# Encoder trunk: four plain columns and nine pairs in the second to fourth feed-forwards, and the residual's sums closer together

## The chip, the cores and the metric

One core of a Trainium2 chip. The time is the device time of one execution in microseconds; the time before is the median of three runs, 2351.93 us (2351.7 to 2353.02).

## The reference

Two layers on a sequence of 512 positions with 1024 channels. Each layer adds a half-step feed-forward, a mixer (state space in layer 0, neighbourhood attention in layer 1), a second half-step feed-forward and a gated input embedding. So there are four feed-forwards, called the first to the fourth here, and only they are changed:

```python
def swiglu(x, w_gu, w_down):                 # w_gu 1024 x 5632, w_down 2816 x 1024
    g, u = jnp.split(x @ w_gu, 2, axis=-1)
    return (jax.nn.silu(g) * u) @ w_down

for i in range(DEPTH):                       # DEPTH = 2
    h = h + 0.5 * swiglu(rmsnorm(h, ffn1_norm[i]), ffn1_w_gu[i], ffn1_w_down[i])
    ...                                      # the mixer
    h = h + 0.5 * swiglu(rmsnorm(h, ffn2_norm[i]), ffn2_w_gu[i], ffn2_w_down[i])
    ...                                      # the gated embedding
```

## The kernel before, in words

The residual h lives in eight tiles of 128 channels by 512 positions. Every float32 matrix product is made of three matmuls: a value is split into a high part (a cast by ScalarE) and a low part (a subtraction by VectorE), and high x high, low x high and high x low are added up in PSUM (`gemm`, line 263). Weights come in units of 128 x 1024: a load on SyncE's queue into one of four raw buffers (`wr`), the cast `wh` (line 218) and the rest `wl` (line 220). `unit` (line 255) keeps up to three split units ready.

The hidden width of 2816 is 22 columns of 128, f=0 to f=21. The kernel computes them in two ways.

*Plain columns* (`gate_up`, line 382). One column takes two units, gate and up, of eight times three matmuls with 512 positions each. Its activation (`activate`, line 413) is a product with the norm's factor R for the gate (VectorE, line 415), a SiLU on ScalarE (416), the same product for up (418), the product of both on GpSimd (419), and a split (ScalarE 286, VectorE 287). R does not stand at the start: the matmuls work on the residual times the gain, and the sum of squares becomes R while TensorE is at the first columns. In the second to fourth feed-forwards R is there within f=1, in the first one within f=2.

*Pairs* (`block`, line 474). Two columns are made of seven half-sized products (a fast 2 x 2 scheme in place of eight), called blocks 0 to 6 here; a product is 24 matmuls with 256 positions (lines 483 to 485). It needs weights that are added up beforehand (lines 240, 243, 245, 251 on VectorE, for each pair) and sums of the residual, made once in each feed-forward by `sums(kk)` (line 432) for the four slices kk = 0 to 3. A slice takes h[kk] and h[kk+4], multiplies both by gain and R (line 437, twice), splits the parts (446 and 447, 286 and 287, 467 and 468) and forms their differences (462 to 465). Block 0 needs line 447's result of all four slices, slice by slice; block 1 needs line 468's.

*Down.* The hidden columns are grouped in chunks. While the products of a chunk run, the downs of the chunk before it are put between them (`ffn_order`, line 47): for each of eight output tiles a unit of weights as wide as the chunk, its matmuls, and an addition to h (line 546).

The columns before the change are chunks (0, 6), (6, 10), (10, 14), (14, 18), (18, 22), in all four feed-forwards: f=0 to 5 are plain, the rest are eight pairs. One slice of sums goes behind each plain column from the one on in which R is there; from f=4 on all that are left go at once. So the second to fourth feed-forwards have the slices behind f=1, 2, 3 and 4, and the first behind f=2, 3 and, two of them, f=4. The loads and splits of weights follow a list in program order (`plan`, line 143). The first pair's four weight blocks and their sums stand in it with the last three plain units (line 161).

The instructions of every engine are put in their final order by a scheduler when the kernel is built; the engines run them in that order.

Of the kernel before, what the change touches and what calls it, by code (L numbers as in the profile page):

```python
# [14 lines left out]
P = 128  # L15
# [3 lines left out]
DEPTH = 2  # L19
FF = 2816  # L20
NF = FF // P
CHUNKS = ((0, 6), (6, 10), (10, 14), (14, 18), (18, 22))
PLAIN = CHUNKS[0][1]
HT = T // 2
EPS = 1e-6
NH = 32
# [19 lines left out]
VAR = (0, 1, 1, 2)  # L46


def ffn_order():

    for f in range(PLAIN):
        yield "plain", f
    for c in range(1, len(CHUNKS)):
        a, b = CHUNKS[c]
        blocks = [(p, i) for p in range(a // 2, b // 2) for i in range(7)]
        d = 0
        for n, (p, i) in enumerate(blocks):
            yield "block", p, i  # L60
            while d < KD and (d + 0.5) * len(blocks) <= KD * (n + 1):
                yield "down", c - 1, d
                d += 1
    yield "between",
    for d in range(KD):
        yield "down", len(CHUNKS) - 1, d


@with_exitstack
def trunk(ctx, tc, A, out):  # L70
    nc = tc.nc
    v, s, g, te, sy = nc.vector, nc.scalar, nc.gpsimd, nc.tensor, nc.sync
# [70 lines left out]
    def plan():  # L143

        for i in range(stop):
            l, w = divmod(i, 4)
            if w in (0, 2):
                gu, gw, dn = [A[f"w_{x}{1 + w // 2}"][l] for x in ("gu", "gw", "dn")]  # L150

                def ahead(p, i_):
                    if i_ == 0:
                        yield "g", [gw[p - PLAIN // 2, x, y] for x, y in ((1, 0), (0, 0), (1, 1), (0, 1))]
                    yield "s", (p, i_)

                for what, *a in ffn_order():
                    if what == "plain":
                        for x in range(2):
                            yield "u", gu[a[0], x]  # L160
                            n = 2 * a[0] + x - (2 * PLAIN - 3)
                            if n >= 0:
                                yield from ahead(PLAIN // 2, n)
                    elif what == "block":
                        yield "o", a
                        if a[1] >= 4 and a[0] < NF // 2 - 1:
                            yield from ahead(a[0] + 1, a[1] - 4)
                    elif what == "down":
                        b = CHUNKS[a[0]]
                        yield "u", dn[a[1], :, b[0] * P:b[1] * P]  # L170
                    elif w == 2:
                        for n in range(2):
                            yield "u", A["w_proj"][l, n]
            elif w == 3:
                for n in range(KD):
                    yield "u", A["w_gate"][l, n]
            elif l % 2 == 0:
                for n in range(65):
                    yield "u", A["w_in"][n]
                for x in range(2):  # L180
                    for d in range(KD):
                        yield "u", A["w_out"][d, :, x * 1024:(x + 1) * 1024]
            else:
                for n in range(24):
                    yield "u", A["w_qkv"][n]
                for d in range(KD):
                    yield "u", A["w_ao"][d]

    todo = list(plan())

    loads = [x for what, a in todo if what in "gu"
# [34 lines left out]
    def prep_next():  # L226
        item = next(todo, None)
        if item is None:
            return False
        what, a = item  # L230
        if what == "u":
            split_raw(*take())
        elif what == "g":
            group[:] = [take()[0] for _ in range(4)]
        elif what == "s":
            p, i = a
            a21, a11, a22, a12 = group
            if i == 0:
                blocks[p] = {0: a11, 2: a21, 3: wide(), 4: a12, 6: a22}
                v.tensor_add(out=blocks[p][3], in0=a21, in1=a22)  # L240
            elif i == 1:
                blocks[p][1] = blocks[p][5] = wide()
                v.tensor_sub(out=blocks[p][1], in0=blocks[p][3], in1=a11)
            else:
                v.tensor_sub(out=a21, in0=a11, in1=a21)
        else:
            p, i = a
            b = blocks[p]
            split_raw(b[i], 1024)
            if i == 1:  # L250
                v.tensor_sub(out=b[5], in0=b[4], in1=b[5])
        top_up()
        return True

    def unit():
        while len(ready) < 3 and prep_next():
            pass
        return ready.pop(0)

    def part(xp, x, cols):  # L260
        return xp[x][:, cols] if isinstance(xp, tuple) else xp[:, x, cols]

    def gemm(pt, w, pairs, first=True, last=True, off=0, cols=slice(0, T), behind=False):
        hi, lo = w
        n = len(pairs)
        for k, xp in enumerate(pairs):
            sl = slice((off + k) * P, (off + k + 1) * P)
            m = te.matmul(out=pt, lhsT=hi[:, sl], rhs=part(xp, 0, cols), start=first and k == 0, stop=False)  # L268
            if behind and k == 0:
                tc.keep_in_program_order(m)  # L270
            te.matmul(out=pt, lhsT=hi[:, sl], rhs=part(xp, 1, cols), start=False, stop=False)  # L271
            te.matmul(out=pt, lhsT=lo[:, sl], rhs=part(xp, 0, cols), start=False, stop=last and k == n - 1)  # L272
# [103 lines left out]
    def ffn(norm, nxt, between=None, first=None):  # L376
        R = [None]
        mids = {}
# [146 lines left out]
            v.tensor_sub(out=hl[1][:, :, c], in0=x, in1=hl[0][:, :, c])  # L525

        made, left = None, [0, 1, 2, 3]
        for what, *a in ffn_order():
            if what == "plain":
                gate_up(a[0])  # L530
                while left and R[0] is not None:
                    sums(left.pop(0))
                    if a[0] < 4:
                        break
            elif what == "block":
                if between and a == [CHUNKS[-1][0] // 2, 0]:
                    next(between)
                block(*a)
            elif what == "between":
                made = between and next(between)  # L540
            else:
                c, d = a
                last = c == len(CHUNKS) - 1
                pt = mm_bank() if last else px_bank()
                gemm(pt, unit(), [mids[f] for f in range(*CHUNKS[c])])
                v.scalar_tensor_tensor(out=h[d], in0=pt, scalar=0.5, in1=h[d], op0=ALU.mult, op1=ALU.add)
                if last:
                    nxt(d)
                    if d == 2 and made is not None:
                        made[1]()  # L550
# [677 lines left out]
    n = Norm(C_G1)  # L1228
# [56 lines left out]
    for i in range(stop):  # L1285
        l, w = divmod(i, 4)
        last = i == stop - 1
        m = None if last else Norm(gains[i + 1], (lambda: md(F32R)) if w == 2 else xa)
        nxt = done if last else m.prep
        if w == 0:  # L1290
            ffn(n, nxt, first=first if i == 0 else None)
        elif w == 1:
            (ssd if l % 2 == 0 else attention)(n, nxt)
        elif w == 2:
            pp = ffn(n, nxt, ple_proj(l))
        else:
            ple(l, n, pp, nxt)
        n = m


def prepare(inp):
    import numpy as np

    def units(w):
        k, n = w.shape[0] // P, w.shape[1] // P
        return w.reshape(k, P, n, P).transpose(2, 1, 0, 3).reshape(n, P, k * P)

    f = {k: np.asarray(a) for k, a in inp.items()}
    o = {}
    o["x"] = f["x"][0].T.reshape(KD, P, T).transpose(1, 0, 2)  # L1310
    p = f["p"][:, 0].reshape(DEPTH, 8, 64, 2, P)
    o["p"] = p.transpose(0, 4, 3, 2, 1).reshape(DEPTH, P, 2, T)
    for i in (1, 2):
        gu = f[f"ffn{i}_w_gu"]
        gu = np.stack([units(gu[l]).reshape(2, NF, P, 1024).transpose(1, 0, 2, 3) for l in range(DEPTH)])
        o[f"w_gu{i}"] = gu[:, :PLAIN]

        gw = gu[:, PLAIN:].reshape(DEPTH, (NF - PLAIN) // 2, 2, 2, P, 2, 512).transpose(0, 1, 3, 5, 4, 2, 6)
        o[f"w_gw{i}"] = gw.reshape(DEPTH, (NF - PLAIN) // 2, 2, 2, P, 1024)
        o[f"w_dn{i}"] = np.stack([units(f[f"ffn{i}_w_down"][l]) for l in range(DEPTH)])  # L1320
    o["w_gate"] = np.stack([units(f["ple_w_gate"][l]) for l in range(DEPTH)])
    o["w_proj"] = np.stack([units(f["ple_w_proj"][l]).reshape(2, 4, P, 256).transpose(0, 2, 1, 3).reshape(2, P, 1024)
                            for l in range(DEPTH)])
# [31 lines left out]
    i = np.arange(P)  # L1355
# [15 lines left out]
    b = np.full((16, 3, 16, 8, 32, 8), NEG, np.float32)  # L1371
# [26 lines left out]
```

## Time and profile before

| | |
|---|---|
| median of 3 runs | 2351.93 us |
| profiled execution, its own time | 2352.96 us |
| span of the profiled execution | 2351.2 us |
| TensorE (PE) busy | 2327.4 us, 99% |
| VectorE (DVE) busy | 1805.7 us, 77% |
| ScalarE (ACT) busy | 1111.8 us, 47% |
| GpSimd (POOL) busy | 353.7 us, 15% |
| mean granted clock of TensorE | 0.997 |

The profile names engines as in the table; SP is SyncE, which issues the loads, and PEld is TensorE's loading of weights, which runs beside its matmuls. L268 is line 268 of the kernel. A row of a timeline gives the start in us, the duration in us, the engine, the line, the operation, what it writes and reads, and, in brackets, how long the engine had been idle and what ended that. Durations of matmuls and of VectorE's instructions overlap with the next one's, so start-to-start times are the price of one in a row of them.

### The profile page before, as it was taken

The numbers are of one execution on the slowest core, as the hardware profiler recorded it, in microseconds if no ns is written. First come the engines' busy times: TensorE is split into PE (matmuls) and PEld (weight loads), VectorE is DVE, ScalarE is ACT, GpSimd is POOL, SyncE is SP. The second block draws the span as 40 slices with busy tenths as digits, with TensorE's granted clock in tenths as the row PEclk, the third lists the DMA queues.
The fourth block names the chain that finished last, engine by engine and source line by source line (L and its number), as shares of the span: only waits on it lengthen the run. The fifth ranks groups of instructions, "written<-read, shape, count | busy, mean of one in ns | idle before, by whom it ended". The sixth has DMA issues, their size and how long they took to land.

```text
span 2351.2 us, 35169 instructions
## 1 busy us (share of the span) xinstructions
PE 2327.4 (99%) x13810; PEld 2026.6 (86%) x13810; DVE 1805.7 (77%) x2565; ACT 1111.8 (47%) x1819; POOL 353.7 (15%) x309
## 2 busy tenths in 40 slices
PE   9999999999999999999999999999999999999998
PEld 8899998888888888899997889999877888999987
DVE  7878868877777747978877897887778757777767
ACT  5433445755655653433345443334437744334353
POOL 1000001444445551100003110000100011000020
PEclk9999999999999999999999999999999999999999
DMA  5233324544444543323322332332433233333222
GB/s 191 84 101 104 108 72 131 172 138 138 143 136 142 162 162 107 115 84 104 108 86 84 103 115 85 104 108 77 145 121 130 103 100 100 111 108 99 81 81 81
DMA packets 99238, 265.95 MB, mean 113 GB/s; under 512 B 12016, under 2 KB 12912, under 8 KB 99072
## 3 DMA queue, kind: packets, MB, share of 16 engines
q1 hardware_dynamic: 98784, 263.57, 34.8%
q8 instruction: 108, 1.77, 0.3%
q14 instruction: 58, 0.48, 0.1%
q10 hardware_dynamic: 288, 0.14, 0.0%
HBM read 253.40 MB, written 10.26 MB: 112 GB/s over the span
## 4 chain that ended last, share of the span: by engine, by line
PE 90%; DVE 5%; ACT 1%; issue 1%; POOL 1%; DMA 1%; SPq 0%; POOLq 0%; ACTq 0%; DVEq 0%
PE ps L268 19%; PE ps L271 19%; PE ps L272 19%; PE ps L485 9%; PE ps L484 9%; PE ps L483 9%; PE ps L866 1%; DVE wl L220 1%; PE ps L844 1%; PE ps L887 1%; PE ps L800 1%; PE ps L786 1%; PE ps L1172 1%; DVE md L290 1%; DVE md L287 1%
## 5 line engine op out<-in xcount | busy, mean ns | idle before, releaser
L268 PE MATMUL ps<-md,wh 128*128 128x512 f32 x2128 | 838.4, 395 | 2.7 <-ACT md L286 2.1
L272 PE MATMUL ps<-md,wl 128*128 128x512 f32 x2128 | 830.7, 391 | 4.7 <-DVE wl L220 4.7
L271 PE MATMUL ps<-md,wh 128*128 128x512 f32 x2128 | 831.3, 391 | 0.7 <-DVE md L290 0.5
L218 ACT CAST wh<-wr 128x1024 fp32r<-128x1024 f32 (+2 forms) x401 | 358.1, 894 | 521.4 <-PE ps L271 199.9
L220 DVE TENSOR_TENSOR wl<-wr,wh 128x1024 fp32r<-128x1024 f32 (+2 forms) x401 | 429.0, 1070 | 114.1 <-ACT wh L218 85.3
L272 PEld LDWEIGHTS ps<-md,wl 128*128 128x128 f32 x2128 | 400.1, 188 | 90.7 <-DVE wl L220 6.7
L268 PEld LDWEIGHTS ps<-md,wh 128*128 128x128 f32 x2128 | 400.5, 188 | 84.4 <-issue 3.5
L271 PEld LDWEIGHTS ps<-md,wh 128*128 128x128 f32 x2128 | 400.9, 188 | 81.1 <-issue 3.3
L314 POOL TENSOR_TENSOR sq<-sq,sq 128x512 f32<-128x512 f32 x71 | 101.1, 1424 | 1444.8 <-ACT sq L310 1444.0
L218 ACT CAST wh<-md 128x1024 fp32r<-128x1024 f32 x160 | 167.7, 1048 | 297.8 <-PE ps L484 263.0
L483 PE MATMUL ps<-sc,wh 128*128 128x256 f32 x896 | 253.8, 283 | 4.2 <-ACT wh L218 4.2
L485 PE MATMUL ps<-sc,wl 128*128 128x256 f32 x896 | 254.3, 284 | 0.8 <-DVE wl L220 0.8
L484 PE MATMUL ps<-md,wh 128*128 128x256 f32 x896 | 254.1, 284 | 0.0
L485 PE MATMUL ps<-md,wl 128*128 128x256 f32 x896 | 254.1, 284 | 0.0
L484 PE MATMUL ps<-sc,wh 128*128 128x256 f32 x896 | 254.1, 284 | 0.0
L483 PE MATMUL ps<-md,wh 128*128 128x256 f32 x896 | 253.9, 283 | 0.0
L489 DVE TENSOR_TENSOR t<-ps,t 128x512 f32<-128x512 f32 x224 | 151.7, 689 | 129.8 <-PE ps L485 127.9
L220 DVE TENSOR_TENSOR wl<-md,wh 128x1024 fp32r<-128x1024 f32 x160 | 196.5, 1228 | 26.8 <-ACT wh L218 26.7
L483 PEld LDWEIGHTS ps<-sc,wh 128*128 128x128 f32 x896 | 172.1, 192 | 8.4 <-ACT wh L218 4.6
L484 PEld LDWEIGHTS ps<-sc,wh 128*128 128x128 f32 x896 | 172.2, 192 | 3.7
L484 PEld LDWEIGHTS ps<-md,wh 128*128 128x128 f32 x896 | 172.4, 192 | 1.2
L483 PEld LDWEIGHTS ps<-md,wh 128*128 128x128 f32 x896 | 172.4, 192 | 1.2
(207 smaller groups left out, 2859.8 us busy)
## 6 DMA issues: line engine op xcount, KB each, us to landing
wr<-in_w_in_dram SPq DMA_DIRECT2D x65, 512.0 KB, 3.5
wr<-in_w_gw_dram SPq DMA_DIRECT2D x64, 512.0 KB, 4.1
md<-in_w_gw_dram SPq DMA_DIRECT2D x64, 512.0 KB, 5.0
wr<-in_w_dn_dram SPq DMA_DIRECT2D x128, 256.0 KB, 2.7
wr<-in_w_gu_dram SPq DMA_DIRECT2D x44, 512.0 KB, 3.5
hs<-crow SPq DMA_DIRECT2D x64, 256.0 KB, 3.9
wr<-in_w_dn_dram SPq DMA_DIRECT2D x32, 384.0 KB, 3.1
wr<-in_w_qkv_dram SPq DMA_DIRECT2D x24, 512.0 KB, 3.7
```

Source lines behind the costliest of these rows:

```text
L218: splits.append(s.copy(out=hi[:, :n], in_=raw[:, :n]))
L220: v.tensor_sub(out=lo[:, :n], in0=raw[:, :n], in1=hi[:, :n])
L268: m = te.matmul(out=pt, lhsT=hi[:, sl], rhs=part(xp, 0, cols), start=first and k == 0, stop=False)
L271: te.matmul(out=pt, lhsT=hi[:, sl], rhs=part(xp, 1, cols), start=False, stop=False)
L272: te.matmul(out=pt, lhsT=lo[:, sl], rhs=part(xp, 0, cols), start=False, stop=last and k == n - 1)
L287: v.tensor_sub(out=dst[:, 1, :], in0=src, in1=dst[:, 0, :])
L290: v.scalar_tensor_tensor(out=dst[:, 1, :], in0=src, scalar=gain, in1=dst[:, 0, :], op0=ALU.mult, op1=ALU.subtract)
L314: (v if fast else g).tensor_add(out=self.acc, in0=self.acc, in1=q)
L483: te.matmul(out=o, lhsT=hi[:, sl], rhs=xh, start=j == 0 and kk == 0, stop=False)
L484: te.matmul(out=o, lhsT=hi[:, sl], rhs=xl, start=False, stop=False)
L485: te.matmul(out=o, lhsT=lo[:, sl], rhs=xh, start=False, stop=j == 1 and kk == 3)
L489: v.tensor_add(out=k[to], in0=pt, in1=k[other])
```

## The change

The second to fourth feed-forwards get chunks of their own: four plain columns and nine pairs, the first chunk of pairs three pairs long. The first keeps its chunks. The number of slices that go behind a plain column is now one in the first feed-forward, and f, at most two, in the others: one slice behind f=1, two behind f=2, and what is left behind the last plain column. In the first feed-forward the fourth slice moves by this from f=4 to f=5. The weights are laid out for it on the host.

```diff
-CHUNKS = ((0, 6), (6, 10), (10, 14), (14, 18), (18, 22))
-PLAIN = CHUNKS[0][1]
+FIRST = ((0, 6), (6, 10), (10, 14), (14, 18), (18, 22))
+OTHERS = ((0, 4), (4, 10), (10, 14), (14, 18), (18, 22))
...
-def ffn_order():
+def ffn_order(chunks):
-    for f in range(PLAIN):
+    for f in range(chunks[0][1]):
         yield "plain", f
...
+                chunks = FIRST if i == 0 else OTHERS
+                plain = chunks[0][1]
...
-                            n = 2 * a[0] + x - (2 * PLAIN - 3)
+                            n = 2 * a[0] + x - (2 * plain - 3)
                             if n >= 0:
-                                yield from ahead(PLAIN // 2, n)
+                                yield from ahead(plain // 2, n)
...
         made, left = None, [0, 1, 2, 3]
-        for what, *a in ffn_order():
+        chunks = FIRST if first else OTHERS
+        for what, *a in ffn_order(chunks):
             if what == "plain":
                 gate_up(a[0])
-                while left and R[0] is not None:
+                n = 1 if first else min(a[0], 2)
+                while left and R[0] is not None and n:
                     sums(left.pop(0))
-                    if a[0] < 4:
-                        break
+                    n -= a[0] < chunks[0][1] - 1
```

The lines of the feed-forward move by 3 or 4: 415, 418, 437, 447 and 483 are 418, 421, 440, 450 and 486 after it.

VectorE in the second feed-forward, before, around f=2: the last rows of the second slice (h tiles hs1509 and hs1545), then f=2's activation, then the third slice (hs1518 and hs1554):

```order
L465 TENSOR_TENSOR t21626_9090<-t21619_9078,t21625_9089 128x256
L468 TENSOR_TENSOR sc1622_9086<-t21625_9089,sc1621_9085 128x512
L220 TENSOR_TENSOR wl1635_9137<-wr1611_9011,wh1634_9135 128x1024
L468 TENSOR_TENSOR sc1624_9088<-t21626_9090,sc1623_9087 128x512
L415 TENSOR_TENSOR t21637_9165<-ps1627_9099,rt1586_8930 128x512
L418 TENSOR_TENSOR t21638_9168<-ps1628_9100,rt1586_8930 128x512
L437 SCALAR_TENSOR_TENSOR t21640_9174<-hs1518_8578,cst_77,rt1586_8930 128x512
L437 SCALAR_TENSOR_TENSOR t21641_9176<-hs1554_8754,cst_77,rt1586_8930 128x512
L287 TENSOR_TENSOR md1639_9171<-t21638_9168,md1639_9171 128x512
```

The same engine and place after the change; the names of the h tiles are the same:

```order
L466 TENSOR_TENSOR t21632_9102<-t21625_9090,t21624_9088 128x256
L467 TENSOR_TENSOR t21631_9101<-t21625_9090,t21631_9101 128x256
L440 SCALAR_TENSOR_TENSOR t21633_9111<-hs1518_8578,cst_77,rt1588_8934 128x512
L468 TENSOR_TENSOR t21632_9102<-t21625_9090,t21631_9101 128x256
L471 TENSOR_TENSOR sc1628_9098<-t21631_9101,sc1627_9097 128x512
L440 SCALAR_TENSOR_TENSOR t21634_9113<-hs1554_8754,cst_77,rt1588_8934 128x512
L471 TENSOR_TENSOR sc1630_9100<-t21632_9102,sc1629_9099 128x512
L450 TENSOR_TENSOR md1635_9115<-t21633_9111,md1635_9115 128x256
```

The third slice now follows inside the second, with no column's activation and no unit's split between them.

TensorE in the second feed-forward, before, where the products begin: the last three matmuls of f=5 (into ps1673) and the first three of block 0 (into ps1684):

```order
L268 MATMUL ps1673_9299<-md1566_8805,wh1659_9238 128x512
L271 MATMUL ps1673_9299<-md1566_8805,wh1659_9238 128x512
L272 MATMUL ps1673_9299<-md1566_8805,wl1660_9240 128x512
L483 MATMUL ps1684_9372<-sc1598_8984,wh1674_9301 128x256
L484 MATMUL ps1684_9372<-sc1599_8985,wh1674_9301 128x256
L485 MATMUL ps1684_9372<-sc1598_8984,wl1675_9303 128x256
```

After the change: the last matmul of f=3 (into ps1644), then block 0 (ps1659), block 1 (ps1666) and the first down (ps1670):

```order
L275 MATMUL ps1644_9136<-md1566_8805,wl1619_9051 128x512
L486 MATMUL ps1659_9225<-sc1600_8988,wh1645_9138 128x256
L487 MATMUL ps1659_9225<-sc1601_8989,wh1645_9138 128x256
L486 MATMUL ps1666_9262<-sc1603_8995,wh1647_9166 128x256
L487 MATMUL ps1666_9262<-sc1604_8996,wh1647_9166 128x256
L271 MATMUL ps1670_9293<-md1594_8972,wh1660_9226 128x512
L274 MATMUL ps1670_9293<-md1594_8972,wh1660_9226 128x512
L488 MATMUL ps1659_9225<-sc1600_8988,wl1646_9140 128x256
```

Block 0 no longer runs in one piece: two matmuls of it, of block 1 and of the first down each stand ahead of its third. Before, all 24 matmuls of block 0 stood behind one another. After it, the first matmul that reads the fourth slice stands behind 18 matmuls of 256 positions and two of 512, counted from the end of f=3.

More of the change, by code (lines that the diff above doesn't have):

```diff
@@ L46 @@
 VAR = (0, 1, 1, 2)
-def ffn_order():
-    for f in range(PLAIN):
+def ffn_order(chunks):
+    for f in range(chunks[0][1]):
         yield "plain", f
-    for c in range(1, len(CHUNKS)):
-        a, b = CHUNKS[c]
+    for c in range(1, len(chunks)):
+        a, b = chunks[c]
         blocks = [(p, i) for p in range(a // 2, b // 2) for i in range(7)]
@@ L65, in ffn_order @@
     for d in range(KD):
-        yield "down", len(CHUNKS) - 1, d
+        yield "down", len(chunks) - 1, d
 @with_exitstack
@@ L149, in plan @@
             if w in (0, 2):
-                gu, gw, dn = [A[f"w_{x}{1 + w // 2}"][l] for x in ("gu", "gw", "dn")]
+                gu, gw, dn = [A[f"w_{x}{2 * l + w // 2}"] for x in ("gu", "gw", "dn")]
+                chunks = FIRST if i == 0 else OTHERS
+                plain = chunks[0][1]
                 def ahead(p, i_):
                     if i_ == 0:
-                        yield "g", [gw[p - PLAIN // 2, x, y] for x, y in ((1, 0), (0, 0), (1, 1), (0, 1))]
+                        yield "g", [gw[p - plain // 2, x, y] for x, y in ((1, 0), (0, 0), (1, 1), (0, 1))]
                     yield "s", (p, i_)
-                for what, *a in ffn_order():
+                for what, *a in ffn_order(chunks):
                     if what == "plain":
@@ L168, in plan @@
                     elif what == "down":
-                        b = CHUNKS[a[0]]
+                        b = chunks[a[0]]
                         yield "u", dn[a[1], :, b[0] * P:b[1] * P]
@@ L527, in ffn @@
         made, left = None, [0, 1, 2, 3]
-        for what, *a in ffn_order():
+        chunks = FIRST if first else OTHERS
+        for what, *a in ffn_order(chunks):
             if what == "plain":
                 gate_up(a[0])
-                while left and R[0] is not None:
+                n = 1 if first else min(a[0], 2)
+                while left and R[0] is not None and n:
                     sums(left.pop(0))
-                    if a[0] < 4:
-                        break
+                    n -= a[0] < chunks[0][1] - 1
             elif what == "block":
-                if between and a == [CHUNKS[-1][0] // 2, 0]:
+                if between and a == [chunks[-1][0] // 2, 0]:
                     next(between)
@@ L542, in ffn @@
                 c, d = a
-                last = c == len(CHUNKS) - 1
+                last = c == len(chunks) - 1
                 pt = mm_bank() if last else px_bank()
-                gemm(pt, unit(), [mids[f] for f in range(*CHUNKS[c])])
+                gemm(pt, unit(), [mids[f] for f in range(*chunks[c])])
                 v.scalar_tensor_tensor(out=h[d], in0=pt, scalar=0.5, in1=h[d], op0=ALU.mult, op1=ALU.add)
@@ L1314, in prepare @@
         gu = f[f"ffn{i}_w_gu"]
[L1315 to L1320, printed above, removed]
+        for l in range(DEPTH):
+            k = 2 * l + i - 1
+            plain = (OTHERS if k else FIRST)[0][1]
+            g_ = units(gu[l]).reshape(2, NF, P, 1024).transpose(1, 0, 2, 3)
+            o[f"w_gu{k}"] = g_[:plain]
+            gw = g_[plain:].reshape((NF - plain) // 2, 2, 2, P, 2, 512).transpose(0, 2, 4, 3, 1, 5)
+            o[f"w_gw{k}"] = gw.reshape((NF - plain) // 2, 2, 2, P, 1024)
+            o[f"w_dn{k}"] = units(f[f"ffn{i}_w_down"][l])
     o["w_gate"] = np.stack([units(f["ple_w_gate"][l]) for l in range(DEPTH)])
```

## The prediction

> **What bounds the kernel now.** I read the page first: how busy each engine is, and which engine the last-ending chain of waits runs through.
>
> ```profile
> PE 2327.4 (99%) x13810; PEld 2026.6 (86%) x13810; DVE 1805.7 (77%) x2565; ACT 1111.8 (47%) x1819; POOL 353.7 (15%) x309
> PE 90%; DVE 5%; ACT 1%; issue 1%; POOL 1%; DMA 1%; SPq 0%; POOLq 0%; ACTq 0%; DVEq 0%
> ```
>
> TensorE is the bound, and it hardly ever waits. Two things can change the time: the matmul work, and new waits of TensorE. Next, what TensorE waits for at all (waits of PE: total, times, longest).
>
> ```profile
> PE ps L272 <- DVE wl L220: 4.7, 3, 2.1
> PE ps L483 <- ACT wh L218: 4.2, 1, 4.2
> ```
>
> The second row is the one to remember: the first product of a pair (L483) once waits 4.2 us. Narrowing the window puts it in the first feed-forward, at the step from plain columns to pairs. In the other three feed-forwards that step costs nothing. This is the step that the change moves.
>
> **The gain: matmuls.** The timeline of PE around that step in the second feed-forward (start, duration): a plain column's last unit, then the first product.
>
> ```profile
> 984.65 0.39 PE L272 MATMUL ps<-md,wl 128*128 128x512 f32 x1
> ...
> 989.41 0.39 PE L272 MATMUL ps<-md,wl 128*128 128x512 f32 x1
> 989.63 0.28 PE L483 MATMUL ps<-sc,wh 128*128 128x256 f32 x1
> ...
> 991.43 0.28 PE L483 MATMUL ps<-sc,wh 128*128 128x256 f32 x1
> ```
>
> Durations overlap, so the price of a matmul is start to start: 21 steps in 4.76 us, 0.2267 us at 512 columns (wide); 15 steps in 1.80 us, 0.120 us at 256 (narrow). Two plain columns are 4 units of 24 matmuls: 96 x 0.2267 = 21.76 us. A pair is 7 products of 24 half-wide matmuls: 168 x 0.120 = 20.16 us. Each of three feed-forwards trades one for the other: **-1.6 us each, -4.8 us in all**. The down matmuls keep their number, and the other layout of the weights is made on the host, outside the time.
>
> The Trainium skill (TensorE: Matmul & The Clock Gate, Back-to-back issue gap) prices an isolated warm matmul at its columns over 2.4 plus 2.5 ns. By it two columns would be 20.7 us and a pair 18.3, an estimate of -2.4 us each and a sum 2.3 us lower. The rows disagree at 256 columns, and I use the rows.
>
> **The price: VectorE's work ahead of the first product.** The products need the sums of the residual (line 432), four slices, and these can only start when the norm's factor is there, in the second column. Before, f=1 to f=4 each brought one slice, and f=5 brought none; now f=1 brings one, f=2 two, f=3 one, and then the products begin. VectorE's timeline in the second feed-forward, before (in brackets, its idle time):
>
> ```profile
> 941.94 0.68 DVE L415 TENSOR_TENSOR t<-ps,rt 128x512 f32<-128x512 f32 x1
> ...
> 945.43 0.69 DVE L287 TENSOR_TENSOR md<-t,md 128x512 fp32r<-128x512 f32 x1 [1.61 <-ACT md L286]
> 946.31 0.69 DVE L418 TENSOR_TENSOR t<-ps,rt 128x512 f32<-128x512 f32 x1 [0.19 <-PE ps L272]
> ...
> 952.06 1.22 DVE L220 TENSOR_TENSOR wl<-wr,wh 128x1024 fp32r<-128x1024 f32 x1
> 953.20 0.41 DVE L465 TENSOR_TENSOR t<-t,t 128x256 f32<-128x256 f32 x1
> 953.53 0.68 DVE L468 TENSOR_TENSOR sc<-t,sc 128x512 fp32r<-128x512 f32 x1
> 954.13 1.22 DVE L220 TENSOR_TENSOR wl<-wr,wh 128x1024 fp32r<-128x1024 f32 x1
> ...
> 957.80 2.45 DVE L437 SCALAR_TENSOR_TENSOR t<-hs,cst,rt 128x512 f32<-128x512 f32 x2
> 960.38 0.69 DVE L287 TENSOR_TENSOR md<-t,md 128x512 fp32r<-128x512 f32 x1
> ...
> 981.10 2.44 DVE L437 SCALAR_TENSOR_TENSOR t<-hs,cst,rt 128x512 f32<-128x512 f32 x2
> 983.46 0.41 DVE L447 TENSOR_TENSOR md<-t,md 128x256 fp32r<-128x256 f32 x1
> ```
>
> The last row is the fourth slice's first result, which block 0 needs for a quarter of its matmuls; it stands at 983.5, and block 0 starts at 989.6. So the step has only 6.2 us to spare before, and the change takes four units, 21.8 us, out ahead of it: without a wait TensorE would be there at 989.63 - 21.76 = 967.9.
>
> When can VectorE be there? Steps from these rows: 1.14 us for 1024 elements (952.06 to 953.20), 0.33 for 256 (953.20 to 953.53), 0.60 for 512 (953.53 to 954.13); a pair of L437 takes 2.58 (957.80 to 960.38), since it runs beside GpSimd's product:
>
> ```profile
> 958.06 1.64 POOL L419 TENSOR_TENSOR t<-t,t 128x512 f32<-128x512 f32 x1 [9.24 <-DVE t L418]
> ```
>
> Without GpSimd beside it L437 steps by 0.66 (73.40 to 74.06, rows below). In the new order, from the first column's product (L418 now) to that result, VectorE has 21 rows of 512, 16 of 256, 8 of 1024 (four splits of weights, and all four sums of the first pair's weights, two of which came later before), three pairs of the residual's products beside GpSimd and one pair alone: 21 x 0.60 + 16 x 0.33 + 8 x 1.14 + 3 x 2.58 + 2 x 0.66 = 36.0 us, and the two waits above, 1.8. From 941.94 that ends at **979.7**. The cover that hid the sums (f=4 and f=5 on TensorE) is gone, and only two columns' activations and their four splits go with it on VectorE.
>
> From 967.9 to 979.7 TensorE lacks the slice for 11.8 us. The new order lets it do 18 narrow matmuls and 2 wide ones ahead of the first that needs the slice: 18 x 0.120 + 2 x 0.2267 = 2.6 us. **Idle: 9.2 us.** Behind that matmul on TensorE's queue lie the rest of blocks 0 and 1 and the first down, so nothing else fills it. On ScalarE the slice's cast stands behind the column's SiLU and its cast, which waits for GpSimd; that costs ScalarE nothing it could use.
>
> A second loss follows. In the first feed-forward, before, the trace shows what such a wait does to the clock (timelines of PE and DVE; then the stretches with start:end, length, PE busy, granted clock):
>
> ```profile
> 74.89 0.28 PE L483 MATMUL ps<-sc,wh 128*128 128x256 f32 x1
> ...
> 79.94 0.58 PE L483 MATMUL ps<-sc,wh 128*128 128x256 f32 x1 [4.19 <-ACT wh L218]
> ...
> 81.55 0.58 PE L485 MATMUL ps<-sc,wl 128*128 128x256 f32 x1 [0.82 <-DVE wl L220]
> 81.93 0.42 PE L483 MATMUL ps<-sc,wh 128*128 128x256 f32 x1
> ...
> 86.20 0.40 PE L485 MATMUL ps<-md,wl 128*128 128x256 f32 x1
> ...
> 90.09 0.28 PE L485 MATMUL ps<-sc,wl 128*128 128x256 f32 x1
> ```
>
> ```profile
> 78.00:80.00 2.00, 0.06 (x1) 0.91 0.00 0
> 84.00:86.00 2.00, 2.00 (x12) 0.50 0.85 213
> 86.00:88.00 2.00, 2.00 (x10) 0.89 0.36 147
> ```
>
> ```profile
> 73.06 0.42 DVE L464 TENSOR_TENSOR t<-t,t 128x256 f32<-128x256 f32 x1
> 73.40 0.74 DVE L437 SCALAR_TENSOR_TENSOR t<-hs,cst,rt 128x512 f32<-128x512 f32 x1
> 74.06 0.41 DVE L465 TENSOR_TENSOR t<-t,t 128x256 f32<-128x256 f32 x1
> ```
>
> After 4.19 us idle the granted clock is 0.50 until about 86.4. From 81.93 to 86.20, 20 steps take 0.2135 us each in place of 0.120: **1.9 us lost**. My waits are longer in sum but broken by short work; I take 1.9 for each, with 0 and 3 as ends.
>
> The Trainium skill (TensorE: Matmul & The Clock Gate, What's actually happening) says that the clock halves after an idle window of about 3.4 us and returns after about as long busy, and that the window runs free. By it a loss is nearer 1.7 us, an estimate; the trace's 79.9 to 86.4 is longer than that, and its row decides.
>
> Each of the three: 9.2 + 1.9 - 1.6 = 9.5 us. They do repeat: first product minus first activation is 47.7 us in the second (941.94, 989.63), and in the third and fourth
>
> ```profile
> 1353.92 0.68 DVE L415 TENSOR_TENSOR t<-ps,rt 128x512 f32<-128x512 f32 x1
> 1401.57 0.28 PE L483 MATMUL ps<-sc,wh 128*128 128x256 f32 x1
> 1953.84 0.68 DVE L415 TENSOR_TENSOR t<-ps,rt 128x512 f32<-128x512 f32 x1
> 2001.53 0.28 PE L483 MATMUL ps<-sc,wh 128*128 128x256 f32 x1
> ```
>
> 47.7 each. **+28.5 us.**
>
> **The first feed-forward changes too.** It keeps six columns, but its fourth slice now comes with f=5, not beside the third at f=4; block 0's weights and f=5's activation go ahead of it. Before, blocks 0 and 1 and the first down (48 narrow, 18 wide matmuls, 9.84 us) start at 74.89 and end 22 steps behind 90.09, at 92.7. Now VectorE's rows from 73.40 to the slice are 1.14 + 0.33 + 0.60 + 1.14 + 0.60 + 0.87 (768 elements, between 0.60 and 1.14) + 0.60 + 0.60 + 2.58 + 0.33 = 8.8 us, so 82.2; TensorE has 38 narrow and 12 wide matmuls left then, 7.3 us: 89.5, or 91.4 at a halved clock. Between -3.2 and -1.3; **-2.3 us**.
>
> **Loads.** The pair's four weight loads are issued four units earlier on SyncE's queue, ahead of f=3's. The raw buffers are four, the group keeps two until its sums are made, so f=3's second load takes the place that this one took before, and lands well ahead of its split at about 957; if it came late it would add up to its landing time.
>
> ```profile
> 942.05 0.33 SPq L201 DMA_DIRECT2D wr<-in_w_gu_dram  x1
> wr<-in_w_gw_dram SPq DMA_DIRECT2D x64, 512.0 KB, 4.1
> ```
>
> I take nothing, with 4.1 us each as the far end. The chunk of three pairs needs VectorE for 11 x 1.14 + 11 x 0.60 and 8/3 x 1.2 of downs, 22.3 us a pair, against TensorE's 20.16 + 8/3 x 12 x 0.2267 = 27.4: no wait.
>
> **Sum.** 28.5 - 2.3 = +26.2 us. The profiled execution is 2352.96 us (span 2351.2), 1.0 above the median of 2351.93; from the median, 2378 us. By ends: waits of 8 to 11 us and a clock loss of 0 to 3 give 2367 to 2388.
>
> **Rivals.**
> *The sums are covered.* VectorE might pull ahead so that the fourth slice is there at 967.9. Then only the gains are left: -4.8 - 2.3, 2345 us. It decides if VectorE's 37.8 us shrink to 26; against it, the two waits are 1.8 us of that, and the rest is busy rows. 5%.
> *A wait no longer than the first feed-forward's.* That step has the same sums, and waits 4.19 + 0.82 us. 5.0 + 1.9 - 1.6 = 5.3, three times 15.9, less 2.3: 2366 us. It decides if VectorE is 4 us quicker than counted; for it, that is the only such wait measured; against it, there the factor comes with three and a half columns still to run, here with two and a half. 11%.
> *The backlog goes on.* VectorE reaches the products late, and ScalarE's and VectorE's splits for blocks 2 and 3 follow in one queue; if one product's time (2.9 us) and another clock loss (1.9) come on top, 4.8 x 3 = 14.4: 2392 us. Against it, 5.1 us of room a pair. 8%.
> My forecast keeps 76%.
>
> **Numbers.** 0.2% is 4.7 us, about what a measurement here can tell from no change. Only the first rival is faster (5%); same 1%; slower 94%. The range 2367 to 2391 holds the forecast and most of the backlog, and leaves out the cover and most of the short wait.
>
> **What would show it.** In the profile after: PE waits at L486 in three places, some 9 us in total each, released by VectorE or ScalarE on the fourth slice (L449, L450); the granted clock at 0.50 for some microseconds behind each; the first feed-forward's wait shorter. I am wrong if TensorE starts block 0 of the second feed-forward without a wait, or if its waits stand elsewhere (loads, later chunks).

## The result and the profile after

The change costs 27.7 us. The median is 2379.59 us (4 runs, 2377.93 to 2380.79) against 2351.9 (4 runs, 2351.7 to 2353.02): 1.0116 times the time before, 95% interval 1.0099 to 1.0134. The profiled execution took 2379.12 us with a span of 2377.3, against 2352.96 and 2351.2: 26.2 us more, where the sum of the prediction was +26.2.

The page of the kernel after, busy time and the engines on the chain that ended last:

```profile
PE 2335.8 (98%) x14026; PEld 2041.5 (86%) x14026; DVE 1835.5 (77%) x2601; ACT 1124.1 (47%) x1831; POOL 344.1 (14%) x303
...
PE 87%; DVE 8%; ACT 1%; POOL 1%; issue 1%; DMA 0%; SPq 0%; POOLq 0%; ACTq 0%; DVEq 0%
```

TensorE is busy for 8.4 us more, although three feed-forwards have less work for it; VectorE's share of the chain goes from 5% to 8%. The time is lost while TensorE waits and runs at a lower clock. Where, the first matmuls of the norms' sums tell, which stand at the ends of the stages. Timelines of PE, before and then after, at the start and the end of the second feed-forward and of the fourth:

```profile
933.36 0.95 PE L328 MATMUL ps<-ones_d,sq 128*128 128x1 f32 x8
1295.60 0.95 PE L328 MATMUL ps<-ones_d,sq 128*128 128x1 f32 x8
1945.25 0.95 PE L328 MATMUL ps<-ones_d,sq 128*128 128x1 f32 x8
2307.50 0.95 PE L328 MATMUL ps<-ones_d,sq 128*128 128x1 f32 x8
```

```profile
930.47 0.95 PE L331 MATMUL ps<-ones_d,sq 128*128 128x1 f32 x8
1302.99 0.95 PE L331 MATMUL ps<-ones_d,sq 128*128 128x1 f32 x8
1960.97 0.95 PE L331 MATMUL ps<-ones_d,sq 128*128 128x1 f32 x8
2333.64 0.95 PE L331 MATMUL ps<-ones_d,sq 128*128 128x1 f32 x8
```

The second feed-forward takes 372.52 us in place of 362.24 (+10.3), the stretch from there to the fourth, which holds the third, 657.98 in place of 649.65 (+8.3), the fourth 372.67 in place of 362.25 (+10.4). All that lies ahead of the second is 2.9 us shorter. So the loss comes three times, once in each feed-forward that was changed. The middle one of these stretches holds more than a feed-forward: from the first matmul of its norm's sums to its last addition the third itself takes 1352.64 to 1701.21, 348.57 us, in place of 1345.30 to 1684.68, 339.38 (+9.2); the mixer behind it is 0.8 us shorter. (The experiments count by the three stretches, and call the mean "the price of a feed-forward": 9.7 us here.)

What PE waits for around the step from plain columns to products in the second feed-forward (935 to 1060 us), where before it waited for nothing:

```profile
PE ps L486 <- ACT md L449: 3.2, 1, 3.2
PE ps L271 <- ACT wh L221: 1.9, 1, 1.9
PE ps L488 <- DVE wl L223: 1.3, 1, 1.3
PE ps L487 <- DVE md L450: 0.2, 1, 0.2
```

And where these waits stand, in the timeline of PE. The first row is the last matmul of f=3, the next the first product, and the last but one ends the first down addition:

```profile
964.76 0.39 PE L275 MATMUL ps<-md,wl 128*128 128x512 f32 x1
964.99 0.28 PE L486 MATMUL ps<-sc,wh 128*128 128x256 f32 x1
...
967.48 0.50 PE L271 MATMUL ps<-md,wh 128*128 128x512 f32 x1 [1.86 <-ACT wh L221]
...
969.52 0.58 PE L488 MATMUL ps<-sc,wl 128*128 128x256 f32 x1 [1.30 <-DVE wl L223]
...
976.33 0.58 PE L486 MATMUL ps<-md,wh 128*128 128x256 f32 x1 [3.21 <-ACT md L449]
...
985.10 0.39 PE L275 MATMUL ps<-md,wl 128*128 128x512 f32 x1
985.33 0.28 PE L486 MATMUL ps<-sc,wh 128*128 128x256 f32 x1
```

Products and the down in these rows are 48 narrow and 12 wide matmuls, 48 x 0.120 + 12 x 0.2267 = 8.48 us at full clock. They take 985.33 - 964.99 = 20.34: 11.86 lost. Up to 976.33, where the fourth slice is there at last, 11.34 us hold 18 narrow and 2 wide (2.61 us): 8.73 lost. From there 30 narrow and 10 wide (5.87 us) take 9.00: 3.13 lost, most of it to the clock. The bracketed waits add up to only 6.55, mostly since the few matmuls between them ran at half clock: such time is idle time by another name. Less the 1.6 us that a pair saves, this is the stage's +10.3.

VectorE in the same stretch, after: the first column's product, a pair of the slices' rows (L440), and the fourth slice's first result:

```profile
939.05 0.68 DVE L418 TENSOR_TENSOR t<-ps,rt 128x512 f32<-128x512 f32 x1
...
944.04 2.45 DVE L440 SCALAR_TENSOR_TENSOR t<-hs,cst,rt 128x512 f32<-128x512 f32 x2
...
976.61 0.42 DVE L450 TENSOR_TENSOR md<-t,md 128x256 fp32r<-128x256 f32 x1
```

From 939.05 to 976.61 are 37.56 us, the length of VectorE's work that sets the step. VectorE is busy for all of it but 1.81 us (a wait of 1.62 for ScalarE's cast L289 and one of 0.19 for TensorE, both ahead of the first slice). In the experiments this length is what is followed.

### The profile page after: what moved, and what is told of

It is laid out like the page before. It is cut to its first block, busy times and chain, and to the rows that moved or that the text cites. A ratio compares the mean times of both kernels' runs of the same rounds, so it can differ in the third digit from the quotient of the medians.

```text
span 2377.3 us, 35649 instructions
## 1 busy us (share of the span) xinstructions
PE 2335.8 (98%) x14026; PEld 2041.5 (86%) x14026; DVE 1835.5 (77%) x2601; ACT 1124.1 (47%) x1831; POOL 344.1 (14%) x303
## 4 chain that ended last, share of the span: by engine, by line
PE 87%; DVE 8%; ACT 1%; POOL 1%; issue 1%; DMA 0%; SPq 0%; POOLq 0%; ACTq 0%; DVEq 0%
PE ps L271 17%; PE ps L274 17%; PE ps L275 17%; PE ps L487 10%; PE ps L488 10%; PE ps L486 10%; DVE wl L223 1%; PE ps L870 1%; DVE md L290 1%; PE ps L848 1%; PE ps L891 1%; DVE t L440 1%; POOL t L422 1%; PE ps L804 1%; DVE sc L471 1%
## 5 line engine op out<-in xcount | busy, mean ns | idle before, releaser
L271 PE MATMUL ps<-md,wh 128*128 128x512 f32 (+1 forms) x2032 | 801.4, 395 | 8.9 <-ACT wh L221 5.6
L275 PE MATMUL ps<-md,wl 128*128 128x512 f32 (+1 forms) x2032 | 793.6, 391 | 4.7 <-DVE wl L223 4.7
L274 PE MATMUL ps<-md,wh 128*128 128x512 f32 (+1 forms) x2032 | 794.1, 391 | 1.3 <-DVE md L293 1.1
L221 ACT CAST wh<-wr 128x1024 fp32r<-128x1024 f32 (+2 forms) x395 | 351.9, 892 | 530.5 <-PE ps L274 197.9
L223 DVE TENSOR_TENSOR wl<-wr,wh 128x1024 fp32r<-128x1024 f32 (+2 forms) x395 | 421.3, 1067 | 114.7 <-ACT wh L221 85.9
L275 PEld LDWEIGHTS ps<-md,wl 128*128 128x128 f32 x2032 | 382.2, 188 | 87.3 <-DVE wl L223 7.0
L221 ACT CAST wh<-md 128x1024 fp32r<-128x1024 f32 x175 | 183.5, 1049 | 312.9 <-PE ps L487 278.8
L486 PE MATMUL ps<-md,wh 128*128 128x256 f32 x980 | 279.7, 285 | 11.2 <-ACT md L449 11.2
L488 PE MATMUL ps<-sc,wl 128*128 128x256 f32 x980 | 281.3, 287 | 5.5 <-DVE wl L223 5.4
L487 PE MATMUL ps<-md,wh 128*128 128x256 f32 x980 | 280.2, 286 | 1.5 <-DVE md L450 1.5
L487 PE MATMUL ps<-sc,wh 128*128 128x256 f32 x980 | 279.4, 285 | 0.0
L488 PE MATMUL ps<-md,wl 128*128 128x256 f32 x980 | 279.3, 285 | 0.0
L486 PE MATMUL ps<-sc,wh 128*128 128x256 f32 x980 | 278.9, 285 | 0.0
L223 DVE TENSOR_TENSOR wl<-md,wh 128x1024 fp32r<-128x1024 f32 x175 | 213.7, 1221 | 21.8 <-ACT wh L221 21.5
L488 PEld LDWEIGHTS ps<-sc,wl 128*128 128x128 f32 x980 | 190.6, 194 | 7.6 <-DVE wl L223 7.6
L487 PEld LDWEIGHTS ps<-md,wh 128*128 128x128 f32 x980 | 190.2, 194 | 4.3 <-DVE md L450 2.7
L486 PEld LDWEIGHTS ps<-sc,wh 128*128 128x128 f32 x980 | 190.1, 194 | 3.6
```

The source lines that it names most:

```text
L221: splits.append(s.copy(out=hi[:, :n], in_=raw[:, :n]))
L223: v.tensor_sub(out=lo[:, :n], in0=raw[:, :n], in1=hi[:, :n])
L486: te.matmul(out=o, lhsT=hi[:, sl], rhs=xh, start=j == 0 and kk == 0, stop=False)
L487: te.matmul(out=o, lhsT=hi[:, sl], rhs=xl, start=False, stop=False)
L488: te.matmul(out=o, lhsT=lo[:, sl], rhs=xh, start=False, stop=j == 1 and kk == 3)
```

## The experiments

The theory: TensorE reaches the products before VectorE has made the fourth slice; the price is VectorE's work from the first column to that slice, less the columns that cover it, and a lower clock behind the wait. Rivals: the slices' closeness is the cause; the clock is the larger part; or the latency of ScalarE's and GpSimd's steps rather than the amount of VectorE's work. Each run is compared with the kernel before timed on the same chip, which is why the time before differs a little from one experiment to the next.

**The new rule for the slices without the new chunks.** Six plain columns everywhere.

```diff
-OTHERS = ((0, 4), (4, 10), (10, 14), (14, 18), (18, 22))
+OTHERS = FIRST
```

> Six plain columns and eight pairs everywhere, as before; only the new rule for the slices stays (first feed-forward: the fourth behind f=5; the others: one behind f=1, two behind f=2, one behind f=3). Theory (the lost columns are the cover, the spacing alone costs nothing): only the first feed-forward's gain is left, 2.5 us, so 2349.4 us. Rival (the sums closer together cost by themselves, wherever the columns end): slower than 2351.9, by up to 10 us for each of three feed-forwards.

Measured: 2353.87 us (11 runs) against 2353.17 before on that chip, ratio 1.0004 (0.9995 to 1.0013). The large loss is gone, so it belongs to the missing columns and not to the closeness. But the expected small gain did not come either: the first feed-forward's last addition is sooner in the profile (362.45 in place of 366.03), but the three others cost 0.8 to 1.4 us each by their own ends. In the timelines of DVE and of PE in its second feed-forward:

```profile
963.98 0.42 DVE L450 TENSOR_TENSOR md<-t,md 128x256 fp32r<-128x256 f32 x1
...
965.59 1.22 DVE L223 TENSOR_TENSOR wl<-wr,wh 128x1024 fp32r<-128x1024 f32 x1
```

```profile
966.86 0.51 PE L275 MATMUL ps<-md,wl 128*128 128x512 f32 x1 [0.52 <-DVE wl L223]
```

A later column's split of weights queues behind the slices, and TensorE waits 0.52 us for it. Products start without a wait. Closeness costs about 1 us, not 10.

**Four columns, one slice behind each of f=1 and f=2.** The last column gets two.

```diff
-                n = 1 if first else min(a[0], 2)
+                n = 1
```

> Four plain columns and nine pairs as after, but one slice behind f=1, one behind f=2 and two behind f=3. Theory (VectorE is busy without a gap, so the amount of its work sets when the fourth slice is there, not the order): within 1 us of the changed kernel in each of three feed-forwards, 2377 to 2383 us. Rival (the closer spacing is what keeps the wait short): one slice's time of 5.6 us more in each, 2396 us.

Measured: 2380.68 us (4 runs), ratio 1.0115 (1.0101 to 1.0129). The timeline of DVE gives the length again:

```profile
941.93 0.68 DVE L418 TENSOR_TENSOR t<-ps,rt 128x512 f32<-128x512 f32 x1
...
979.48 0.42 DVE L450 TENSOR_TENSOR md<-t,md 128x256 fp32r<-128x256 f32 x1
```

37.55 us, and a price of 9.5 us a feed-forward. With four columns this other order of VectorE's rows changes nothing: their amount is the same, and so is the price.

**TensorE kept busy.** 76 matmuls into a bank that nobody reads stand between f=3 and the products, to hold the clock.

```diff
+                if not first and a[0] == chunks[0][1] - 1:
+                    idle_ = px_bank()
+                    x_ = xs[0][0][0]
+                    for _ in range(76):
+                        te.matmul(out=idle_[:, :HT], lhsT=x_[:, :P], rhs=x_, start=True, stop=True)
```

> The changed kernel with 76 matmuls of 256 positions into an unused bank between f=3 and block 0 of the second to fourth feed-forwards, 9.1 us of filling for TensorE that nobody reads. Theory (part of the loss is the halved clock behind the wait): the clock stays at 1.0, about 1.4 us less in each, in the third less, 2375 to 2377 us. Rival (the clock plays no part, all is waiting): 2379 to 2381, or above it if the filling delays the products.

Measured: 2381.58 us (4 runs), ratio 1.0119 (1.0104 to 1.0135): missed, no gain. The clock did stay up (stretches of the second feed-forward: start:end, length, PE busy, granted clock, DMA), and the timeline of PE shows why it did not pay:

```profile
964.00:974.00 10.00, 10.00 (x69) 1.00 0.05 7
...
978.00:986.00 8.00, 6.61 (x48) 1.00 0.28 90
```

```profile
968.17 9.28 PE L543 MATMUL ps<-sc 128*128 128x256 f32 x76
...
979.53 0.39 PE L486 MATMUL ps<-md,wh 128*128 128x256 f32 x1 [1.01 <-ACT md L449]
```

The first matmul that needs the slice is as late as ever, 979.53 - 968.17 = 11.36 us behind f=3 (11.34 after). Of real work, only 9 narrow matmuls stand in that time, 1.08 us, where the kernel after does 2.61: the scheduler put less of it ahead of the wait. 1.5 us of what the clock gave went there. The second and fourth feed-forward, at +9.7, are some 0.6 below the kernel after, the third 0.5 above (1355.27 to 1704.35, 349.08 us, +9.7 against before, like the other two); and the stretch ahead of the second, whose code is that of the kernel after, ended 3.2 us later than there (last section), which ate the rest. By this run TensorE at full clock still loses 9.7 + 1.6 = 11.3 us a feed-forward, 10.28 (11.36 - 1.08) up to the slice and 1.0 behind it, where the kernel after lost 3.13: by this sum the clock is worth some 2.1 us, though the time of the run does not show it, and the rival that it is the larger part is out.

**Less work on VectorE.** The first pair of the three feed-forwards takes raw weight blocks in place of the sums of blocks. The run leaves these sums out for that pair and so changes what is computed.

```diff
-            if i == 0:
+            if p == 2:
+                if i == 0:
+                    blocks[p] = {0: a11, 1: a12, 2: a21, 3: a22, 4: a12, 5: a12, 6: a22}
+            elif i == 0:
...
-            if i == 1:
+            if i == 1 and p != 2:
```

> The changed kernel, where the first pair of the second to fourth feed-forwards takes its raw weight blocks in place of their sums: four VectorE instructions of 1.14 us fewer ahead of the fourth slice (this pair's columns are another product). Theory (VectorE's work sets the start of the products, one for one): 4.6 us less waiting in each, 13.7 us in all, 2366 us, a little less if the clock recovers sooner. Rival (TensorE waits for loads, for ScalarE's queue or for GpSimd's product): 2377 to 2380 us.

Measured: 2370.25 us (4 runs), ratio 1.007 (1.0056 to 1.0083): 17.1 us above before on that chip, where the change itself is 27.7 above. That is 10.6 us less, of 13.7 expected. The timeline of DVE (lines are 3 higher):

```profile
941.28 0.68 DVE L421 TENSOR_TENSOR t<-ps,rt 128x512 f32<-128x512 f32 x1
...
956.54 0.69 DVE L424 TENSOR_TENSOR t<-ps,rt 128x512 f32<-128x512 f32 x1 [0.65 <-PE ps L278]
...
975.25 0.42 DVE L453 TENSOR_TENSOR md<-t,md 128x256 fp32r<-128x256 f32 x1
```

The length is 33.97 us, 3.6 less (expected 4 x 1.14 = 4.6), and the price 5.9 us, 3.8 less than after. Of the missing 1.0, 0.65 is the middle row's wait, which the kernel after does not have: with less to do VectorE was at f=2's activation before TensorE had finished that column. One us less of the length ahead of the slice is about one us less of the feed-forward. The steps on ScalarE and GpSimd are untouched here, so the rival that their latency alone sets the price is out.

**GpSimd's product on VectorE.** VectorE gets more rows, but its sums no longer run beside GpSimd.

```diff
-            g.tensor_mul(out=um, in0=um, in1=gm)
+            v.tensor_mul(out=um, in0=um, in1=gm)
```

> The changed kernel with the plain columns' product of SiLU and up on VectorE in place of GpSimd (line 422). Theory (GpSimd's product makes VectorE's pairs of L440 slower: 2.58 us beside it, 1.32 alone): four products of 0.60 us more and three pairs 1.26 us shorter, 1.4 us sooner for the fourth slice in each of three feed-forwards, up to 3 with the two waits behind GpSimd gone: 2371 to 2376 us. Rival (the long pair is VectorE's own and GpSimd only happens to run then): 2.4 us later in each, 2387 us.

Measured: 2374.67 us (4 runs) against 2352.72 before on that chip, ratio 1.0095 (1.0081 to 1.0109). The timeline of DVE in this run and, behind it, two of GpSimd's rows in the kernel after, the second of which belongs to the pair at 944.04 above:

```profile
938.23 0.68 DVE L418 TENSOR_TENSOR t<-ps,rt 128x512 f32<-128x512 f32 x1
...
943.22 0.74 DVE L440 SCALAR_TENSOR_TENSOR t<-hs,cst,rt 128x512 f32<-128x512 f32 x1
943.88 0.68 DVE L422 TENSOR_TENSOR t<-t,t 128x512 f32<-128x512 f32 x1
944.48 0.74 DVE L440 SCALAR_TENSOR_TENSOR t<-hs,cst,rt 128x512 f32<-128x512 f32 x1
...
973.78 0.41 DVE L450 TENSOR_TENSOR md<-t,md 128x256 fp32r<-128x256 f32 x1
```

```profile
940.56 1.30 POOL L422 TENSOR_TENSOR t<-t,t 128x512 f32<-128x512 f32 x1 [18.04 <-ACT t L419]
944.26 1.67 POOL L422 TENSOR_TENSOR t<-t,t 128x512 f32<-128x512 f32 x1 [2.40 <-DVE t L421]
```

A row of L440 takes 0.74 us where a pair of them took 2.45. With four more products on VectorE the length still falls to 35.55 us, 2.0 less, and the price to 7.9, 1.8 less. (0.4 of the 2.0 are shorter waits of VectorE over that length, 1.44 us in place of 1.81.) The Trainium skill (SBUF — State Buffer, SBUF: two separate sides) says that VectorE, with two inputs from SBUF, and GpSimd, reading there, share a pair of ports that one instruction holds to its end while the other is blocked. The trace agrees: after, GpSimd's row ends at 944.26 + 1.67 = 945.93 and the pair at 944.04 + 2.45 = 946.49, 0.56 later, about the step of one row of L440 alone (943.22 to 943.88, 0.66). And one row of L440, GpSimd's product where VectorE was mostly idle (1.30 at 940.56) and the other row add up to 0.66 + 1.30 + 0.66 = 2.62, an estimate of the three one after the other; the pair's step after is 2.58 (944.04 to 946.62).

**The first feed-forward's change alone.** The chunks of before, and only its fourth slice behind f=5.

```diff
-OTHERS = ((0, 4), (4, 10), (10, 14), (14, 18), (18, 22))
+OTHERS = ((0, 6), (6, 10), (10, 14), (14, 18), (18, 22))
...
-                n = 1 if first else min(a[0], 2)
+                n = 1 if first else 1 + 3 * (a[0] >= 4)
```

> The kernel before with one thing of the change: the first feed-forward's fourth slice behind f=5 in place of f=4; the second to fourth are as before. Theory (the first feed-forward gains by itself, 2.0 to 3.6 us by the ends of its last addition in the runs so far): 2349.5 us. Rival (that gain is chance of the clock): 2351.9, as before.

Measured: 2351.43 us (11 runs) against 2352.72, ratio 0.9995 (0.9986 to 1.0004): not told from nothing, though in its profile the first feed-forward ends 3.3 us sooner. The edit's worth alone stays open. (The second and fourth feed-forward, which this run leaves as before, take 362.26 and 362.27 us in place of 362.24 and 362.25: these stages repeat closely.)

**The columns the other way.** As in the last experiment, with eight plain columns and seven pairs in the first feed-forward.

```diff
-FIRST = ((0, 6), (6, 10), (10, 14), (14, 18), (18, 22))
+FIRST = ((0, 8), (8, 10), (10, 14), (14, 18), (18, 22))
```

> As e6_first_late, and the first feed-forward with eight plain columns and seven pairs: the change turned round, where the wait is. Theory (matmuls of two columns cover the sums): its wait and clock loss before, 8.0 us, go, and 1.6 us of matmuls come: 6.4 us faster than before, 2345.5 us. Rival (the wait moves to another place, the loads or the buffers of the eight columns): 2352 or slower.

Measured: 2346.47 us (8 runs), ratio 0.9973 (0.9963 to 0.9983). It beats both kernels, by 6.25 us against before on that chip. Against the last experiment, which shares the fourth slice behind f=5, it is 4.96 us faster; that part is the two columns'. The theory used forward: with two columns more, TensorE waits nowhere at that step. The first feed-forward's last addition in the timelines of DVE: before, after, and this one:

```profile
366.03 0.68 DVE L546 SCALAR_TENSOR_TENSOR hs<-ps,hs 128x512 f32<-128x512 f32 x1
```

```profile
363.68 0.68 DVE L550 SCALAR_TENSOR_TENSOR hs<-ps,hs 128x512 f32<-128x512 f32 x1
```

```profile
358.70 0.68 DVE L550 SCALAR_TENSOR_TENSOR hs<-ps,hs 128x512 f32<-128x512 f32 x1
```

That is 7.3 us sooner than before, and 4.0 sooner than in the last experiment (362.69): the whole gain lies in this stage.

## Why the prediction was right

The length of VectorE's work and the price of a feed-forward (mean of three, against before) over the kernels with four columns:

| kernel | length, us | price, us |
|---|---|---|
| after | 37.56 | 9.7 |
| one slice a column | 37.55 | 9.5 |
| product on VectorE | 35.55 | 7.9 |
| raw blocks | 33.97 | 5.9 |

2.0 us less length is 1.8 us less price, and 3.6 is 3.8, by two different edits. That VectorE's work is what ends last is shown. That it is exactly one for one is not: single feed-forwards of one kernel differ by up to 1.2 us (9.2 to 10.4 after, taking the third by its own ends).

- *VectorE's work:* 37.8 us predicted, 37.56 measured. The slice was to come 11.8 us behind f=3; it came 976.61 - 964.99 = 11.6 behind it. Both stand 3 us sooner than predicted, since the first feed-forward and its mixer end sooner.
- *Idle time:* 9.2 predicted, 8.73 lost up to the slice. The waits stand in more places than foreseen: only 3.21 + 0.18 us are put to the slice's own rows (L449, L450), where the prediction's sign named some 9. Two others, 1.86 and 1.30 us, are for casts and splits of weights (L221, L223), not for the slice; they lie within the wait for it and cost nothing of their own.
- *The clock:* 1.9 us predicted; 3.13 were lost from the slice on in the second feed-forward, of which the kernel with fillers, at full clock, lost 1.0 too. So the clock's part, 2.1, was about right, and the 1.0 (the wait at L487 and short stalls behind it) was not in the sum; it more than made up for idle time counted 0.5 too large, which is luck.
- *The sum of the three:* +28.5 predicted, 10.3 + 8.3 + 10.4 = +29.0, or +29.9 with the third by its own ends. The feed-forwards cost 1.4 us more than the sum, and the mixers' 0.5 and 0.8 us less made up for it: that the profiled difference meets the forecast to the tenth, +26.2, is luck, and that it lies near is not. The lower end of the range is off by one: the prediction's terms give 2351.93 + 3 x 6.4 - 3.2 = 2368, not 2367.
- *The gain of a pair:* not measured by itself. 11.86 lost and a stage 10.3 longer leave 1.6, the term's size.
- *The first feed-forward:* -2.3 predicted; its last addition comes 366.03 - 363.68 = 2.35 sooner. The fit is luck too: the prediction took the middle between a full and a halved clock, and the same edit alone gave 366.03 - 362.69 = 3.34, with a granted clock of 1.00 from 82 to 84 us where the kernel after had 0.50. Alone, as an edit, the gain was 1.3 us of the whole, inside its interval.
- *Loads and later chunks:* no new wait there, as predicted.

The rivals fall by the same rows. The sums were not covered. A wait as short as the first feed-forward's would have been 5.3 us a feed-forward. No wait follows in blocks 2 and 3.

## What to carry to other kernels

A plain stretch ahead of a clever one may be cover for another engine's preparations: before shortening it, add up what that engine must do from its first possible moment to the result that is needed, row by row, and compare it with what the bound engine has left to do. Below that point a microsecond of cover taken away was lost about one for one here, and the gain per unit, 1.6 us here, is small beside it. The same sum, read the other way, finds where more cover pays: two more columns in the first feed-forward, together with the later fourth slice, gave 6.25 us.

## What the runs showed of the hardware that was not expected

The clock halves during a wait that is broken by work. The stretches of the second feed-forward after (granted clock behind the busy time), and around the third one's wait for the slice:

```profile
966.00:968.00 2.00, 0.52 (x2) 1.00 0.00 0
968.00:970.00 2.00, 0.70 (x3) 0.69 0.00 0
970.00:972.00 2.00, 2.00 (x10) 0.50 0.71 166
...
976.00:978.00 2.00, 1.50 (x5) 0.50 0.00 0
...
980.00:982.00 2.00, 2.00 (x8) 0.50 0.74 211
982.00:984.00 2.00, 2.00 (x16) 0.90 1.03 420
```

```profile
1394.00:1396.00 2.00, 1.30 (x7) 0.64 0.28 115
1396.00:1398.00 2.00, 0.00 (x0) 1.00 0.00 0
1398.00:1400.00 2.00, 1.12 (x4) 0.71 0.00 0
```

No single gap ahead of 970 is longer than 1.86 us, and the clock is at 0.50 by then. In the third feed-forward it came back to 1.00 inside the wait and fell again behind it, and it lost 9.2 us by its own ends where the others lost 10.3 and 10.4. The Trainium skill (TensorE: Matmul & The Clock Gate, What's actually happening) says that the gate watches windows of about 3.4 us that run free of the program; that the same waits meet the clock at another phase agrees with it. In the kernel with fillers, where the clock stayed at 1.00, all three lost 9.7: the 1.1 to 1.2 us between the feed-forwards went with the clock, as far as one other kernel can tell.

Code that no edit touches moves too. In the kernel with fillers the first feed-forward's last addition came at 363.98 us, and the second feed-forward started at 933.65 (timelines of DVE and PE):

```profile
363.98 0.68 DVE L555 SCALAR_TENSOR_TENSOR hs<-ps,hs 128x512 f32<-128x512 f32 x1
```

```profile
933.65 0.95 PE L331 MATMUL ps<-ones_d,sq 128*128 128x1 f32 x8
```

The mixer between them took 569.7 us there, 567.3 before and 566.8 after. With fillers and after, every engine runs the same instructions there in the same order. Most of the 2.9 us between these two arises at one wait (timelines of PE, after and then with fillers):

```profile
818.45 1.14 PE L790 MATMUL ps<-msk,md 128*128 128x128 f32 x8 [1.83 <-ACT md L794]
```

```profile
820.16 1.97 PE L795 MATMUL ps<-msk,md 128*128 128x128 f32 x8 [2.81 <-ACT md L799]
```

Ahead of it the two differ by 0.6 us (816.22 and 816.85), a few matmuls behind it by 2.9 (819.89 and 822.78). The wait was 1 us longer with fillers, and from 820 to 822 us the granted clock was 0.50 there and 1.00 after. Differences of 1 to 3 us in one profiled execution prove nothing about an edit elsewhere.
